# A two-layer hybrid trunk on one core: input groups projected in another order, key selection beside the gates, weight pieces ordered behind the splits of activations

## The chip, the cores and the metric

The kernel runs on one core of one Trainium2 chip. The metric is the device time of one launch in microseconds (us); smaller is better. The inputs lie in HBM as f32, the output goes back there as f32.

## What is computed

A trunk of two layers on one sequence of 256 tokens with 1024 channels. Each layer is `x += 1/2 FFN1(norm(x))`, `x += mixer(norm(x))`, `x += 1/2 FFN2(norm(x))`; a last RMSNorm follows. An FFN is `(silu(g) * u) @ w_down` with `g, u = split(h @ w_gu)` and 2816 hidden columns. The mixer is, cut to what matters:

```
(q_a,k_a,v_a,f_a, q_b,k_b,v_b, q_c,c_kv, q_i,k_i,w_i, gates) = split(h @ w_in)
y_a = forgetting_attention(6 heads)         # softmax with a forget bias
y_b = stick_breaking_attention(5 heads)
k_c, v_c = split(rmsnorm(c_kv) @ w_kv_up)
score = sum_h relu(q_i @ k_i) * w_i         # the indexer, 4 heads
sel   = top_k(score, 64)                    # key selection
y_c = dsa_attention(5 heads over the selected keys)
merged = sum over a, b, c of sigmoid(gate) * (y @ w_up)
return merged @ w_out
```

## The kernel before

**Tiling.** All weight matrices are streamed once, as f32 chunks `raw` (1024 KB or less) that SyncE's queue loads into four buffers. Each chunk is cut into pieces of up to 128x1024; `emit_piece` (L258) calls `split` (L249) for each, which makes two fp16 parts: ScalarE writes `whi` (L251), then VectorE writes the rest, `wlo` (L253). Fourteen pieces of each may stand ready (`HL_BUFS`); `advance` keeps that many ahead of TensorE in program order. A product takes three fp16 matmuls (weights' high part by the activation's high part `xThi` and low part `xTlo`, weights' low part by `xThi`), all in `project_T` (L339, weights stationary, 256 columns moving) or `project` (L374 to L376). Before the kernel's main stream ends, nearly all of TensorE's time goes there.

**Banks.** The products accumulate in four PSUM banks, two for a group of 512 output columns, so a group can start only when the group before the last one has been read out of its two banks. In an FFN the gate columns `g` are read by `gate(k)` (L655 to L662: `s` = `g` times the norm's row `R`, then Silu), the up columns `u` by L667. `gate` is tried ahead of each contraction step k of the `u` columns. In the first FFN, whose norm `R` comes late, it waits for step 6 if `R` isn't there yet.

**Mixer.** `IN_GROUPS` (L50) lists the column groups of `w_in` in the order in which they are projected: QI (indexer), VA (values and forget logits of the first heads), QC (sparse heads and latent), KA, QA, QB, QB2, VB. After each, tasks are made: generators that issue a bit of attention work at every step. `background()` (L307) steps them once or so for each weight piece, so that attention stands between the matmuls of the projections. The tasks are `indexer` (scores `is`, then eight rounds of top-k on VectorE, L915 and L916, then the mask `pen`), `forget`, `latent`, `fox_heads` (names ending in a), `stick_heads` (b), `dsa_heads` (c, which finishes the indexer and the latent first). In their names, `s` is a score matmul, `p` a softmax, `pp`/`pT` its transpose, `y` the value product, `c` the stick-breaking sums, `e` and `l` their logarithms. The indexer's rounds wait until the first heads have begun (`while "fox" not in X`). After the eight groups the six gate groups `gt0` to `gt5` follow, then the 12 sigmoids (L1162), the up-projections `up` of the three branches (evacuated at L1174, summed at L1177, split into `mT`), and `w_out` (matmuls `o`, which read `mT`).

**Norms.** `ss` (sum of squares by matmul), `gms`, a power on GpSimd, `rstd`, `dg` (a diagonal), `rb` (a matmul that spreads it into a row) and `R`.

**What sets the order.** A scheduler fixes at build time the order of the instructions of each engine, by dependences and by the order in which the code issues them; `behind` adds an ordering without data. At run time each engine takes its instructions in that order. The profile names the FFN tiles without layer (`gw_ffn_gu`, `s0w_ffn_gu`), the order views with one.

## Time and profile before

| | us |
|---|---|
| timed runs | 1142.18, 1143.40, 1143.76 |
| median | 1143.4 |
| profiled execution, its own time | 1145.33 |
| its span | 1143.5 |
| TensorE (PE) busy | 1113.5 (97%) |
| VectorE (DVE) busy | 799.3 (70%) |
| ScalarE (ACT) busy | 649.8 (57%) |

The profile is of one execution. An engine is busy while one of its instructions runs; the shares are means over stages that differ. A row of the view of waits gives, for an engine's line, what released it at last, the idle time in all, how many times, and the longest.

### The profile page before, as it was taken

Reading aid. Unit: us, or ns where it says so; the run is one execution under the profiler, and the core shown is the slowest. Engines: PE = TensorE matmul, PEld = TensorE weight load, DVE = VectorE, ACT = ScalarE, POOL = GpSimd, SP = SyncE. Lnnn points to the kernel's source line nnn. Section 1 sums busy time; section 2 is a strip of 40 time slices with the busy share of each in tenths; the row PEclk is TensorE's granted clock in tenths of the full one; section 3 lists DMA queues with packets and bytes.
Section 4 is the critical chain, followed back from the end, with each engine's and each line's share of the span. In section 5 each row is a group of like instructions: output and inputs, shape, how many; then the busy total and the mean of one; then the engine's idle time right before and its main releaser. Section 6 shows DMA issues by size and latency. Waiting matters only on the chain.

```text
span 1143.5 us, 23671 instructions
## 1 busy us (share of the span) xinstructions
PE 1113.5 (97%) x9746; PEld 960.4 (84%) x9746; DVE 799.3 (70%) x1757; ACT 649.8 (57%) x1040; POOL 12.5 (1%) x25
## 2 busy tenths in 40 slices
PE   9999999999999899999999999999999999999996
PEld 8888887778888788888888888868788888888765
DVE  6966656898677876575676575579976789666733
ACT  7845545677667464464454464466766766644520
POOL 1000000000000000000000000000000000000000
PEclk9999999999999899999999999999999999999998
DMA  9956655555343765577656476556533448556801
GB/s 316 368 174 217 227 172 174 161 182 176 111 139 112 244 223 164 181 231 235 199 186 183 151 238 200 178 168 190 180 130 111 148 148 295 176 165 197 256 1 41
DMA packets 118762, 210.02 MB, mean 184 GB/s; under 512 B 4802, under 2 KB 43892, under 8 KB 118644
## 3 DMA queue, kind: packets, MB, share of 16 engines
q1 hardware_dynamic: 118324, 207.88, 56.1%
q8 instruction: 78, 1.28, 0.5%
q10 hardware_dynamic: 320, 0.53, 0.1%
q14 instruction: 40, 0.33, 0.1%
HBM read 207.35 MB, written 1.05 MB: 182 GB/s over the span
## 4 chain that ended last, share of the span: by engine, by line
PE 77%; DVE 13%; ACT 6%; issue 2%; DMA 1%; POOL 0%; POOLq 0%; DVEq 0%; ACTq 0%
PE gw_ffn_gu L339 19%; PE uw_ffn_gu L339 19%; PE d512w_ffn_down L339 8%; PE d0w_ffn_down L339 8%; PE gt L339 6%; DVE wlo L253 5%; PE o L339 3%; ACT whi L251 2%; PE in L376 2%; PE in L374 1%; PE in L375 1%; DMA raw<-in_w_ffn_gu_dram 1%; ACT gt L1162 1%; PE in L339 1%; DVE gt L1174 1%
## 5 line engine op out<-in xcount | busy, mean ns | idle before, releaser
L253 DVE SCALAR_TENSOR_TENSOR wlo<-raw,whi 128x1024 f16<-128x1024 f32 (+6 forms) x425 | 476.2, 1128 | 258.7 <-ACT whi L251 255.5
L251 ACT ACTIVATE whi<-raw 128x1024 f16<-128x1024 f32 (+6 forms) x425 | 411.4, 978 | 378.9 <-PE uw_ffn_gu L339 93.4
L339 PEld LDWEIGHTS <-whi 128*128 128x128 f16 x5504 | 537.7, 98 | 72.1 <-issue 8.3
L339 PEld LDWEIGHTS <-wlo 128*128 128x128 f16 x2768 | 271.2, 98 | 34.2 <-issue 1.8
L339 PE MATMUL gw_ffn_gu<-xThif,whi 128*128 128x256 f16 x704 | 191.8, 273 | 2.0 <-DVE s0w_ffn_gu L660 1.4
L339 PE MATMUL gw_ffn_gu<-xThif,wlo 128*128 128x256 f16 x704 | 191.5, 273 | 0.6 <-DVE wlo L253 0.6
L339 PE MATMUL uw_ffn_gu<-xThif,wlo 128*128 128x256 f16 x704 | 191.9, 273 | 0.0
L339 PE MATMUL uw_ffn_gu<-xThif,whi 128*128 128x256 f16 x704 | 191.9, 273 | 0.0
L339 PE MATMUL uw_ffn_gu<-xTlof,whi 128*128 128x256 f16 x704 | 191.9, 273 | 0.0
L339 PE MATMUL gw_ffn_gu<-xTlof,whi 128*128 128x256 f16 x704 | 191.7, 273 | 0.0
L339 PE MATMUL gt<-xThimx,whi 128*128 128x256 f16 x384 | 104.8, 273 | 0.0
L339 PE MATMUL gt<-xThimx,wlo 128*128 128x256 f16 x384 | 104.7, 273 | 0.0
L339 PE MATMUL gt<-xTlomx,whi 128*128 128x256 f16 x384 | 104.7, 273 | 0.0
L339 PE MATMUL d0w_ffn_down<-ahw_ffn_gu,whi 128*128 128x256 f16 x264 | 72.0, 273 | 0.0
L339 PE MATMUL d0w_ffn_down<-alw_ffn_gu,whi 128*128 128x256 f16 x264 | 72.0, 273 | 0.0
L339 PE MATMUL d512w_ffn_down<-alw_ffn_gu,whi 128*128 128x256 f16 x264 | 72.0, 273 | 0.0
L339 PE MATMUL d512w_ffn_down<-ahw_ffn_gu,wlo 128*128 128x256 f16 x264 | 72.0, 273 | 0.0
L339 PE MATMUL d0w_ffn_down<-ahw_ffn_gu,wlo 128*128 128x256 f16 x264 | 72.0, 273 | 0.0
L339 PE MATMUL d512w_ffn_down<-ahw_ffn_gu,whi 128*128 128x256 f16 x264 | 72.0, 273 | 0.0
L339 PE MATMUL o<-mT,whi 128*128 128x256 f16 x256 | 45.1, 282 | 4.2 <-ACT mT L251 3.2
L339 PE MATMUL in<-xThimx,whi 128*128 128x256 f16 x176 | 48.0, 273 | 0.0
L339 PE MATMUL in<-xThimx,wlo 128*128 128x256 f16 x176 | 48.0, 273 | 0.0
(329 smaller groups left out, 1400.7 us busy)
## 6 DMA issues: line engine op xcount, KB each, us to landing
raw<-in_w_ffn_gu_dram SPq DMA_DIRECT2D x61, 1024.0 KB, 5.4
raw<-in_w_ffn_down_dram SPq DMA_DIRECT2D x39, 1024.0 KB, 5.1
raw<-in_w_in_dram SPq DMA_DIRECT2D x26, 1024.0 KB, 5.0
raw<-in_w_ffn_gu_dram SPq DMA_DIRECT2D x32, 768.0 KB, 4.6
raw<-in_w_in_dram SPq DMA_DIRECT2D x12, 768.0 KB, 4.5
raw<-in_w_out_dram SPq DMA_DIRECT2D x8, 1024.0 KB, 5.1
raw<-in_w_ffn_down_dram SPq DMA_DIRECT2D x7, 512.0 KB, 3.8
raw<-in_w_in_dram SPq DMA_DIRECT2D x4, 896.0 KB, 4.8
```

The costliest lines, as they stand in the source:

```text
L251: a = nc.scalar.activation(hv, src, AF.Copy, scale=scale)
L253: return a, nc.vector.scalar_tensor_tensor(lv, src, scale, plain(hv), op0=ALU.mult, op1=ALU.subtract, **more)
L339: m = nc.tensor.matmul(o, u, v[:, k, :], start=(k == 0 and q == 0 and b % 2 == 0), stop=(end and q == len(ops) - 1))
L374: nc.tensor.matmul(o, a, wh, start=(k == 0), stop=False)
L375: nc.tensor.matmul(o, a, wl, start=False, stop=False)
L376: state["last"] = nc.tensor.matmul(o, b, wh, start=False, stop=(k == lastk))
L1162: i = behind(nc.scalar.activation(v, v, AF.Sigmoid), *(exps if sig0 is None else [sig0]))
L1174: nc.vector.scalar_tensor_tensor(v, pair(ps[i], 2), 1.0 / (sw * sy), v, op0=ALU.mult, op1=ALU.mult)
```

## The change

Four parts. (1) The groups are projected in the order VA, KA, QA, QB, QB2, VB, QI, QC, and the tasks of the indexer, the latent and the sparse heads are made after their groups, that is after those of the first and the stick-breaking heads. (2) The indexer steps three times, not twice, ahead of each pair of score heads, the wait for the first heads is gone, and the second pair of the first heads starts five steps late rather than three. (3) `state["urgent"]`: the split of the next weight piece is ordered behind the last parts of a norm, and behind the split of `mT`, on either engine. (4) `gate` is forced from step 3 in the first FFN and from step 4 elsewhere, where it was step 6. The same work is issued as before.

```diff
-IN_GROUPS = [(QI, 324), (VA, 390), (QC, 448), (KA, 384), (QA, 384), (QB, 384), (QB + 384, 256), (VB, 320)]
+IN_GROUPS = [(VA, 390), (KA, 384), (QA, 384), (QB, 384), (QB + 384, 256), (VB, 320), (QI, 324), (QC, 448)]
...
         r = split(hv, lv, src, sw, guard and guard.weight())
+        for own, first in zip(r, state.pop("urgent", ())):
+            behind(own, first)
...
-                    self.parts(k, xT[:, k, :])
+                    state["urgent"] = self.parts(k, xT[:, k, :])
...
-                if s or (norm.R is None and k < 6):
+                if s or (norm.R is None and k < (3 if isinstance(norm, FirstNorm) else 4)):
...
-                yield
-                yield
+                for _ in range(3):
+                    yield
...
-            while "fox" not in X:
-                yield
...
-            X["fox"] = True
...
-        group(*IN_GROUPS[0], [(0, 324, False, PQI)])
-        t_idx = Task(indexer(), True)
-        group(*IN_GROUPS[1], [(0, WA + HA, False, PVA)])
+        group(*IN_GROUPS[0], [(0, WA + HA, False, PVA)])
         t_f = Task(forget(), True)
-        group(*IN_GROUPS[2], [(0, WC, True, PQC), (WC, P, False, PCKV)])
-        t_lat = Task(latent(), True)
         norm.need(True)
-        for g, at, eighth in ((3, 3, False), (4, 0, True)):
+        for g, at, eighth in ((1, 3, False), (2, 0, True)):
...
-            Task(later(fox_heads(hs, f"a{l}"), 3 * (i == 1)))
-        for hs in pairs(HC):
-            Task(dsa_heads(hs, f"c{l}"))
+            Task(later(fox_heads(hs, f"a{l}"), 5 * (i == 1)))
...
         for hs in pairs(HB):
             Task(stick_heads(hs, f"b{l}"))
+        group(*IN_GROUPS[6], [(0, 324, False, PQI)])
+        t_idx = Task(indexer(), True)
+        group(*IN_GROUPS[7], [(0, WC, True, PQC), (WC, P, False, PCKV)])
+        t_lat = Task(latent(), True)
+        for hs in pairs(HC):
+            Task(dsa_heads(hs, f"c{l}"))
...
-                            split(mh[:, k:k + 2, :], ml[:, k:k + 2, :], v0, sm, note())
+                            state["urgent"] = split(mh[:, k:k + 2, :], ml[:, k:k + 2, :], v0, sm, note())
```

Three places where the order of instructions differs follow; a row is line, operation, written tile <- read tiles, shape.

**First FFN, VectorE.** Here `s0` and `s1` are the two gate reads of the first chunk and `wlo15` to `wlo18` pieces of the stream. Before:

```order
L253 SCALAR_TENSOR_TENSOR wlo15_301,sums_71<-raw11_294,whi15_300 128x1024
L660 TENSOR_TENSOR s0w_ffn1_gu0_0_483<-gw_ffn1_gu0_0_0_172,Rf1_0_486 128x512
L253 SCALAR_TENSOR_TENSOR wlo16_307,sums_71<-raw12_304,whi16_306 128x1024
L253 SCALAR_TENSOR_TENSOR wlo17_311,sums_71<-raw12_304,whi17_310 128x1024
L660 TENSOR_TENSOR s1w_ffn1_gu0_0_490<-gw_ffn1_gu0_0_1_173,Rf1_0_486 128x512
L667 TENSOR_TENSOR s0w_ffn1_gu0_0_483<-uw_ffn1_gu0_0_0_388,s0w_ffn1_gu0_0_483 128x512
```

Changed:

```order
L253 SCALAR_TENSOR_TENSOR wlo15_301,sums_71<-raw11_294,whi15_300 128x1024
L253 SCALAR_TENSOR_TENSOR wlo16_307,sums_71<-raw12_304,whi16_306 128x1024
L253 SCALAR_TENSOR_TENSOR wlo17_311,sums_71<-raw12_304,whi17_310 128x1024
L662 TENSOR_TENSOR s0w_ffn1_gu0_0_436<-gw_ffn1_gu0_0_0_172,Rf1_0_439 128x512
L662 TENSOR_TENSOR s1w_ffn1_gu0_0_443<-gw_ffn1_gu0_0_1_173,Rf1_0_439 128x512
L253 SCALAR_TENSOR_TENSOR wlo18_349,sums_71<-raw13_314,whi18_348 128x1024
```

`s0` has moved from behind `wlo15` to behind `wlo17`, and `s1` stands right after it.

**Mixer of the first layer, VectorE, key selection.** `m8` are the maxima of a round, `isc` the scores. Before, two of the eight rounds:

```order
L915 MAX m80_0_1_3058<-isc0_2612 128x8
L915 MAX m80_128_1_3061<-isc0_2612 128x8
L253 SCALAR_TENSOR_TENSOR wlo107_3037,sums_71<-raw58_2837,whi107_3036 128x1024
L916 MATCH_REPLACE isc0_2612<-m80_0_1_3058,isc0_2612 128x128
L916 MATCH_REPLACE isc0_2612<-m80_128_1_3061,isc0_2612 128x256
L915 MAX m80_0_2_3088<-isc0_2612 128x8
L915 MAX m80_128_2_3091<-isc0_2612 128x8
L253 SCALAR_TENSOR_TENSOR wlo108_3065,sums_71<-raw59_2897,whi108_3064 128x1024
L916 MATCH_REPLACE isc0_2612<-m80_0_2_3088,isc0_2612 128x128
```

Changed, the last round and what follows it:

```order
L915 MAX m80_0_7_3747<-isc0_3531 128x8
L915 MAX m80_128_7_3750<-isc0_3531 128x8
L916 MATCH_REPLACE isc0_3531<-m80_0_7_3747,isc0_3531 128x128
L916 MATCH_REPLACE isc0_3531<-m80_128_7_3750,isc0_3531 128x256
L850 TENSOR_TENSOR kcT0_3758<-kcTp0_3755,kcT0_3758 64x256
L919 TENSOR_SCALAR pen0_3753<-isc0_3531 128x384
L821 TENSOR_TENSOR Tc00_3766<-qc00_3763,Tc00_3766 64x256
L812 TENSOR_TENSOR gt0_2371<-gt0_0_1_3442,Rmx_0_2462 128x512
L253 SCALAR_TENSOR_TENSOR wlo119_3777,sums_71<-raw64_3318,whi119_3776 128x1024
```

Before, the rounds stand between pieces and other attention work; in the changed program all eight stand in one row of 32, behind the last `isc` sum, ahead of the mask `pen`, of `Tc00` (operand of the sparse heads' first score `sc00`) and of the read of the gate bank `gt0_0_1`. No piece stands between `wlo118` ahead of this block and `wlo119` behind it.

**End of the gates, ScalarE.** `gt0` is sigmoid in place (the gate tile of layer 0), `eb` and `y0` are the last stick-breaking steps. Before:

```order
L786 ACTIVATE eb04_4440<-eb04_4440 128x384
L1162 ACT_TABLE_LOAD
L1162 ACTIVATE gt0_2371<-gt0_2371 128x512 x3
L251 ACTIVATE y0_2989<-yb04_4545 64x256
L1162 ACTIVATE gt0_2371<-gt0_2371 128x512 x9
L251 ACTIVATE whi139_4568<-raw74_4280 128x1024
```

Changed:

```order
L1160 ACT_TABLE_LOAD
L1160 ACTIVATE gt0_2371<-gt0_2371 128x512
L251 ACTIVATE whi130_4267<-raw70_4035 128x1024
L1160 ACTIVATE gt0_2371<-gt0_2371 128x512 x4
L251 ACTIVATE whi131_4309<-raw70_4035 128x512
L1019 COPY pTc04_4303<-ppc04_4299 128x384
L1160 ACTIVATE gt0_2371<-gt0_2371 128x512 x3
L251 ACTIVATE whi132_4343<-raw71_4110 128x1024
L251 ACTIVATE y0_2712<-yc04_4337 64x256
L251 ACTIVATE whi133_4373<-raw71_4110 128x512
L251 ACTIVATE whi134_4401<-raw72_4211 128x1024
L251 ACTIVATE whi135_4435<-raw72_4211 128x512
```

The 12 sigmoids stood in one row behind the last attention work, ahead of `whi139`; now ten stand between pieces from `whi130` on and two behind `whi139`. Further on, the second `mT` pair moved from behind `whi151` to between `whi150` and `whi151`.

## Rows read from the trace of the kernel before

**Rows 1.** The page's chain of work that ended last, by engine.

```profile
PE 77%; DVE 13%; ACT 6%; issue 2%; DMA 1%; POOL 0%; POOLq 0%; DVEq 0%; ACTq 0%
```

**Rows 2.** Waits of PE: reader <- releaser: us in total, times, longest.

```profile
PE sa L860 <- ACT pa L786: 4.5, 2, 2.2
PE o L339 <- ACT mT L251: 3.2, 2, 2.7
PE is L860 <- DVE Tiq L819: 2.2, 2, 1.1
...
PE sc L860 <- ACT pa L786: 1.7, 2, 0.9
...
PE sb L860 <- DVE eb L1101: 1.3, 2, 0.7
PE o L339 <- DVE mT L253: 1.0, 2, 0.6
PE yc L990 <- ACT pTc L1019: 0.7, 2, 0.3
PE ya L990 <- ACT pTa L1019: 0.7, 2, 0.4
```

**Rows 3.** Windows: stretch, length, busy PE, PEld, DVE, ACT, POOL, granted clock, DMA share, GB/s.

```profile
30.00:36.00 6.00, 3.98 (x36) 3.27 (x34) 6.00 (x11) 5.90 (x9) 0.00 (x0) 1.00 1.01 355
250.17:253.59 3.42, 3.42 (x17) 2.35 (x17) 3.42 (x17) 2.47 (x5) 0.00 (x0) 0.50 0.58 159
379.88:386.70 6.82, 5.80 (x27) 3.88 (x27) 6.18 (x13) 3.13 (x5) 0.00 (x0) 0.50 0.37 111
813.37:816.78 3.41, 3.41 (x15) 2.18 (x14) 3.41 (x13) 2.13 (x5) 0.00 (x0) 0.50 0.85 264
```

**Rows 4.** Timeline of PE, first FFN: start, us, ..., [idle before <- releaser].

```profile
32.61 0.27 PE L339 MATMUL gw_ffn_gu<-xThif,whi 128*128 128x256 f16 x1 [1.37 <-DVE s0w_ffn_gu L660]
...
35.50 0.27 PE L339 MATMUL gw_ffn_gu<-xThif,whi 128*128 128x256 f16 x1 [0.65 <-DVE s1w_ffn_gu L660]
```

**Rows 5.** Timeline of DVE, first FFN.

```profile
31.87 0.68 DVE L660 TENSOR_TENSOR s0w_ffn_gu<-gw_ffn_gu,Rf 128x512 f32<-128x512 f32 x1
32.48 1.21 DVE L253 SCALAR_TENSOR_TENSOR wlo<-raw,whi 128x1024 f16<-128x1024 f32 x1
...
34.76 0.69 DVE L660 TENSOR_TENSOR s1w_ffn_gu<-gw_ffn_gu,Rf 128x512 f32<-128x512 f32 x1
```

**Rows 6.** Timeline of ACT, from the sigmoids to `w_out`, layer 0.

```profile
351.57 4.78 ACT L1162 ACTIVATE gt<-gt 128x512 f32<-128x512 f32 x9
...
377.96 2.00 ACT L251 ACTIVATE whi<-raw 128x1024 f16<-128x1024 f32 x2 [7.37 <-DMA raw<-in_w_ffn_gu_dram]
379.87 1.13 ACT L251 ACTIVATE mT<-gt 128x512 f16<-128x512 f32 x2
```

**Rows 7.** Timeline of SP's queue ahead of `w_out`, layer 0.

```profile
358.59 16.90 SPq L238 DMA_DIRECT2D raw<-in_w_ffn_gu_dram  x4
```

**Rows 8.** Timeline of DVE at two norms: mixer's of layer 0, then FFN2's.

```profile
193.98 0.22 DVE L533 TENSOR_SCALAR gms<-ssmx 128x1 f32<-128x1 f32 x2
...
195.86 0.48 DVE L547 TENSOR_SCALAR dgmx<-ident,rstdmx 128x128 f32<-128x128 f32 x2
...
412.01 0.17 DVE L544 TENSOR_SCALAR rstdf<-rstdf 128x2 f32<-128x2 f32 x1 [0.80 <-POOL rstdf L473]
```

**Rows 9.** Timeline of DVE, one round of top-k, layer 0.

```profile
229.51 0.61 DVE L915 MAX8 m<-isc 128x8 f32<-128x128 f32 x2
...
232.09 0.09 DVE L916 MATCH_VALUE_LOAD isc<-m,isc 128x8 f32 x1
...
232.42 0.41 DVE L916 MATCH_REPLACE8 isc<-m,isc 128x256 f32<-128x256 f32 x1
```

**Rows 10.** Timeline of PE, two matmuls in succession.

```profile
371.80 0.27 PE L339 MATMUL up<-y,whi 128*128 128x256 f16 x1
371.91 0.27 PE L339 MATMUL up<-y,wlo 128*128 128x256 f16 x1
```

More of the change, by code (lines that the diff above doesn't have):

```diff
@@ L1129, in mixer @@
         for i, hs in enumerate(pairs(HA)):
-            Task(later(fox_heads(hs, f"a{l}"), 3 * (i == 1)))
-        for hs in pairs(HC):
-            Task(dsa_heads(hs, f"c{l}"))
-        ps = group_T(*IN_GROUPS[5])
+            Task(later(fox_heads(hs, f"a{l}"), 5 * (i == 1)))
+        ps = group_T(*IN_GROUPS[3])
         for t in range(NT):
@@ L1139, in mixer @@
         scaled(qk[HD:, 8, :], ps[1][HD:, :SEQ], norm.R[HD:, :], False)
-        ps = group_T(*IN_GROUPS[6])
+        ps = group_T(*IN_GROUPS[4])
         scaled(qk[:, 9:11, :], pair(ps[0], 2), norm.by_row(2), False)
-        group(*IN_GROUPS[7], [(0, WB, False, PVB)])
+        group(*IN_GROUPS[5], [(0, WB, False, PVB)])
         for hs in pairs(HB):
             Task(stick_heads(hs, f"b{l}"))
+        group(*IN_GROUPS[6], [(0, 324, False, PQI)])
[4 more added lines that the diff above has]
+            Task(dsa_heads(hs, f"c{l}"))
         for i in range(6):
```

## The prediction

> **What bounds the kernel now.** I read the chain of work that ended last first: TensorE (PE) carries 77% of it [rows 1], and PE is busy for 97% of the span. The matmuls follow each other at 0.11 us [rows 10] and no part of the change takes one away. So the time can move in two ways only: PE's idle time, and the clock it is granted. The waits of PE come next. Apart from the start and the tail they sum to some 17 us, and the reader is to see that they lie in three places: two gate reads of the first FFN [rows 4], the attention work of both mixers, and the start of the second half of `w_out`, where `o` waits for `mT` [rows 2]. Then the windows: the granted clock is 1.00 (2.4 GHz) nearly everywhere, and 0.50 (1.2 GHz) in three stretches, each right behind a long stop. Two of 3.4 us follow the stops of 2.2 us at `sa`, one of 6.8 us follows the stop of 2.7 us at `o` in layer 0 [rows 2, 3]. A stretch at half clock costs half its length: 1.7 us and 3.4 us. After the 1.37 us stop of the first FFN the clock stays at 1.00 [rows 3, 4]. VectorE (DVE) is the engine most often waited for behind these stops: it never pauses in 30 to 36 us and in 250 to 254 us [rows 3].
>
> I make the sum as changes to the median of 1143.4 us. The profiled execution, 1145.33 us by itself and 1143.5 in its span, is 0.2% above that median; a term of a few us does not feel this.
>
> **First FFN: +5.6 us.** Forcing the gate at step 3 issues `s0` in the code sooner, but on DVE it now stands behind `wlo16` and `wlo17` rather than ahead of them. `wlo16` can't move forward, since `whi16` on ScalarE comes behind the copy of `R` in both programs. So `s0` takes the time slot of `s1`: it starts at about 34.7 us instead of 31.87, and `s1` follows 0.6 us later [rows 5]. The next gate chunk on PE needs the bank that `s0` reads. It began at 32.61 and did its first part until 34.85, where it stopped for `s1` (35.50 less 0.65) [rows 4]. Now it begins at 35.5, so 34.85 - 32.61 = 2.2 us of PE work move behind the stop, which grows from 1.4 to some 4.2 us; the stop for `s1` nearly goes, as its 0.6 us lie beside the first six matmuls. That is longer than any stop in the rows, so I charge the clock of the longest one, 2.7 us with 3.4 us of cost; the low end is 1.7. Together +5.6, at least +2.2 if the clock stays. The other FFNs' first reads show no wait in the trace, and gating them at step 4 is worth nothing; what hides them is that their norms are ready while the group before is projected.
>
> **`w_out`: -6.3 us.** Before, nine of the sigmoids run in one 4.8 us block on ScalarE, from 351.57 on, with `whi139` behind them [rows 6]; DVE has no piece to work on, later it has too much, raw buffers come free late, SP's next load goes out only at 358.59 [rows 7], and ScalarE waits 7.4 us for a load at 377.96 with the last `mT` behind that piece [rows 6]. In the changed order attention ends earlier, ten sigmoids lie between pieces, and the last `mT` stands ahead of `whi151`. I expect the 2.7 + 0.4 us of layer 0 and its 3.4 us of clock to go, and the 1.1 us of layer 1. What is late next is `wlo148`, which DVE takes ahead of the low part of `mT`; layer 1 already shows the stop of this kind, 0.6 us, so I leave 0.65 in each layer. Layer 0: -6.5 + 0.65; layer 1: -1.1 + 0.65; in sum -6.3. Bounds: -7.6 if that also goes, -2 if the loads stay late. Here too `urgent` acts. Its other use, the parts of a norm, gets nothing: PE shows no wait there.
>
> **Mixers, what goes.** The stops of before stand at places that no longer exist in that form. Per layer: `sa` 2.25 with 1.7 of clock, `is` 1.1, `sc` 0.87, `sb` 0.67, `ya` 0.35, `yc` 0.34 [rows 2, 3]: -7.3.
>
> **Mixers, what comes.** (a) Norm row. Before, the whole VA group stood between `ss` and `rb`; now 11 matmuls do, 11 x 0.11 = 1.2 us. From `gms` to the end of `dg` took 193.98 to 196.34 = 2.36 us; so PE waits 1.2 us. At FFN2's norm GpSimd's step left DVE idle for only 0.80 us, and the same steps would take some 0.65 less [rows 8]: 0.5. The neighbours of neither row are those of the changed order; I take 0.9. (b) Key selection. `dsa_heads` finishes the indexer at once, and nothing delays it any longer until the sparse heads are far off. All eight rounds then run in one block. One round is 0.54 us for the two maxima and 0.66 for the two replacements (from start to next start) [rows 9], so 1.2, and eight take 9.6. The relu, the last sum, `kcT`, `pen` and `Tc00` around them are six short steps of 0.3 to 0.4 us, as one MAX8: some 2.3. From `is3` to `sc00` that makes 11.9 us. PE has, between these two in its order, 84 gate matmuls (9.2 us) and `cb04` (some 0.5 by its columns): 9.7. A stop of 2.2 us, just that of `sa`, so its clock too: 3.9; the low end is 0 where DVE comes to the block with `is2` already summed, the high end 5 with another stretch of clock. Pieces don't run out meanwhile: by the order some nine of the fourteen are still ahead of PE. (c) Others. In the changed order attention cuts into the projection at about 25 places, in few matmuls each. At 14 of them, by counting the matmuls that lie between two dependent attention steps, the chain through ScalarE and DVE is longer than PE's work. Before there were five such places besides `sa`, and they stopped PE for 3.3 us, 0.67 each. 14 x 0.67 = 9.4 is the high end; 1.7, five places at the smallest of 0.34, the low one. A stop at one place lets the other engines get ahead for the next, so the 14 can't all count in full; I take half, 4.7.
>
> Per layer 0.9 + 3.9 + 4.7 - 7.3 = +2.2; both layers +4.4.
>
> **Sum.** 5.6 - 6.3 + 4.4 = +3.7: 1147.1 us, forecast 1147.
>
> The Trainium skill, "TensorE: Matmul & The Clock Gate", section "Why this matters for your kernels", lets the clock fall only after stops longer than those of 2.2 and 2.7 us here. By that rule the removed clock at `o` would be worth nothing, the two at `sa` and `sc00` would cancel as they do now, and the sum would be 3.4 us higher, 1150.5. The trace disagrees, 0.50 behind each of the three stops, and the measurement decides.
>
> **Rivals.**
> *Faster, about 1137.* The places of (c) are hidden as before, and the stop at `sc00` falls short of a lower clock: 0.5 + 2.2 + 1.7 - 7.3 = -2.9 per layer, so 5.6 - 6.3 - 5.8 = -6.5. For it: attention now starts earlier and has longer to spread, and before only five such places stopped PE. Against it: DVE is full in 250 to 254 us and its work is the same. It decides if the mixers' sum of new stops is below 7.3 per layer. The Trainium skill, "Perfetto Trace Analysis", section "Optimization Strategy", says that stages bound by different engines gain when they are interleaved. That speaks for this rival, since key selection now lies beside the gates; the order shows a solid block within them, which speaks against it.
> *No change, about 1143.* The mixers come out even, and the first FFN's loss meets `w_out`'s gain: 5.6 - 6.3 = -0.7.
> *Much slower, about 1160.* All places of (c) count, 9.4, and one of them falls together with another to a stop that lowers the clock, 1.7: 0.9 + 3.9 + 9.4 + 1.7 - 7.3 = +8.6 per layer, +17.2 - 0.7. It decides if DVE, rather than PE, sets the pace from QB to the gates.
> *The change doesn't do what it says* in one part already: the gate that is forced earlier is read later.
>
> **How the numbers follow.** A measurement of this kernel can tell about 0.2%, 2.3 us, from no change. Forecast 0.45, from 1141 to 1153 by the ends of its terms; faster rival 0.25; no change 0.15; much slower 0.15. The range takes in the forecast's and nearly all of the two outer rivals': 1137 to 1158, with one in ten left out on either side. Faster by over 0.2%: most of the faster rival with a little of the two middle cases, 0.28. Within 0.2%: most of "no change" and the forecast's lower part, 0.17. Slower: 0.55.
>
> **What would show it.** In the first FFN: PE's wait for `s0` of about 4.2 us and a clock of 0.50 behind it; if it is 2 us or less, that term is wrong. In `w_out`: `o` waiting for `mT` 0.7 us or less in both layers, no 7 us wait of ScalarE for a load, a clock of 1.00. In the mixers: `rb` waiting for `dg` by 0.5 to 1.2 us, `sc` waiting for `Tc` by about 2 us with the eight rounds in one block of 10 us on DVE, and many waits of 0.3 to 1 us at `pp`, `s`, `c` and `y`. If the sum of PE's waits in one mixer is below 5.6 us, the faster rival holds. What would make all of it wrong is a stop at a place where I counted PE's cover as enough, above all a piece that comes too late behind the block.

## The result, and the profile after

The changed kernel takes **1154.4 us** (median of three runs, 1152.80 to 1155.14) against 1143.4: a ratio of 1.0101, with an interval of 1.0085 to 1.0117. It is 11.0 us slower where 3.7 was forecast. Later medians of the kernel before lie at 1141.7 to 1142.2, against which the loss is 12.4 us. The time lies within the range and on the side that was held likelier; the size is three times the forecast, and it is nearer to the 1160 of the rival "much slower" than to 1147.

The page of the changed kernel, its busy times and its chain, answering [rows 1]:

```profile
PE 1125.5 (98%) x9746; PEld 963.9 (84%) x9746; DVE 801.5 (70%) x1757; ACT 649.8 (56%) x1040; POOL 10.2 (1%) x25
...
PE 84%; DVE 9%; ACT 5%; issue 1%; POOL 0%; POOLq 0%; DVEq 0%; ACTq 0%
```

PE's busy time grew from 1113.5 to 1125.5 us, by 12.0, as much as the loss, and no matmul was added. What PE doesn't spend busy went from 30.0 us of the span (1143.5 - 1113.5) to 27.1 (1152.6 - 1125.5). So PE stands idle for less time than before and is slower all the same. Against the second profile of the kernel before (experiment e9: busy 1110.9, not busy 29.2) the two changes are +14.6 and -2.1. That is what has to be explained.

The waits of PE after, answering [rows 2] (reader <- releaser: us in total, times, longest):

```profile
PE sc L862 <- DVE Tc L821: 4.3, 2, 2.1
PE gw_ffn_gu L341 <- DVE s0w_ffn_gu L662: 3.8, 1, 3.8
PE ppa L1017 <- ACT pa L788: 2.5, 4, 0.9
PE warm L428 <- POOL ident masks.py:199: 2.0, 1, 2.0
PE o L341 <- DVE mT L253: 1.3, 2, 0.6
PE rbmx L553 <- DVE dgmx L549: 1.2, 2, 0.6
```

The clock, answering [rows 3] (columns as there): full just ahead of the first FFN's stop, 0.50 (1.2 GHz) in three stretches ahead of the tail, one behind that stop and one behind each stop at `sc`.

```profile
34.00:35.18 1.18, 0.17 (x2) 0.16 (x2) 1.18 (x4) 0.77 (x1) 0.00 (x0) 1.00 1.09 378
35.18:38.59 3.41, 3.41 (x18) 2.45 (x17) 2.90 (x6) 3.38 (x5) 0.00 (x0) 0.50 1.02 381
304.83:308.25 3.42, 3.42 (x19) 2.47 (x18) 3.36 (x6) 0.52 (x1) 0.00 (x0) 0.50 0.23 27
868.03:871.44 3.41, 3.41 (x19) 2.45 (x17) 3.35 (x7) 0.52 (x1) 0.00 (x0) 0.50 0.21 58
```

Where the time went, by the lengths of the stages: from the first PE matmul of one to the first of the next. The first column, the gate and up columns of FFN1, is taken from the start of the span. A mixer's stage begins with the `w_down` of the FFN1 ahead of it, which takes 57.64 us before and after alike, and ends at the first `up`; the length of a mixer given below is that of this stage, unless a window is named. The row "before again" is a second profile of the kernel before (experiment e9); the changes are taken against it.

| us | FFN1 (gate, up) | `w_down`, mixer 0 | up, `w_out` 0 | FFN2, next FFN1 (gate, up) | `w_down`, mixer 1 | up, `w_out` 1 |
|---|---|---|---|---|---|---|
| before, the profile of the rows | 128.03 | 222.59 | 48.90 | 290.85 | 222.59 | 44.26 |
| before again | 128.21 | 222.56 | 44.25 | 290.84 | 223.64 | 44.25 |
| after | 131.28 | 228.66 | 43.59 | 290.69 | 228.67 | 43.59 |
| change | +3.07 | +6.10 | -0.66 | -0.15 | +5.03 | -0.66 |

In sum +12.7, about the 12.4 of the medians; what comes behind these stages is 0.2 us shorter. The mixers hold 11.1 of it.

Now one mixer in both profiles: windows from the norm's `ss` to the first `up`, layer 0, first of the kernel before and then of the changed one (columns as in [rows 3]).

```profile
192.36:350.62 158.26, 152.62 (x1288) 127.13 (x1287) 127.74 (x347) 108.87 (x239) 3.24 (x3) 0.99 0.50 157
```

```profile
196.86:359.94 163.08, 158.26 (x1287) 128.71 (x1287) 126.79 (x346) 113.22 (x248) 2.08 (x3) 0.99 0.48 154
```

Idle is the length less PE's busy time: 5.64 us before, 4.82 after. The clock's mean is the same, 0.99. Busy time grew by 5.64 us with as many matmuls, and with fewer columns: of two groups of columns, each projected ahead of `ss`, the changed kernel leaves out of its window VA (7.94 us), the kernel before QI (6.69), so on equal terms the stretch is 6.1 longer, not 4.8.

To see what "busy" hides I took the time from each PE start to the next, less the shortest tenth of that kind of matmul (the same for both kernels), and put what is left to a stop (the trace shows PE idle), to half clock, or, where neither applies, to the rest:

| mixer 0, us | stops | half clock | rest |
|---|---|---|---|
| before | 6.78 | 1.66 | 8.23 |
| after | 6.68 | 1.67 | 14.43 |

The whole loss of the mixer, 6.2 us, is in the rest. Where the line between stop and rest is drawn moves up to 1.8 us from one column to the other; the rest grows by some 6 us in any case. There it lies at the matmuls of attention and those around them: `yc` 1.47 to 2.71, `ya` 1.43 to 2.51, `yb` 1.37 to 1.92, `cb` 0.35 to 1.10, `pp` 0.01 to 1.02. What changed for them is their company. I call it a visit when matmuls of one kind of tile stand in a row on PE. A mixer had 85 such rows before, among them 9 visits of value products `y`; it has 122 after, 17 of them of `y`. The projection itself is interrupted hardly more often, 44 times against 41; what grew are the changes within these interruptions. Two visits on PE's timeline (start, duration); the kernel before has all twelve value matmuls of a pair of heads in one, between two gate matmuls:

```profile
281.09 0.27 PE L339 MATMUL gt<-xThimx,wlo 128*128 128x256 f16 x1
281.29 1.15 PE L990 MATMUL ya<-pTa,pr 128*64 128x128 f32 x12
282.37 0.28 PE L339 MATMUL gt<-xThimx,whi 128*128 128x256 f16 x1
```

In the changed kernel a pair is cut up, with transposes `pp` of another pair between:

```profile
247.55 0.30 PE L378 MATMUL in<-whi,xTlomx 128*128 128x324 f16 x1
247.82 0.33 PE L1017 MATMUL ppa<-ident,pa 128*128 128x128 f32 x1
248.08 0.43 PE L990 MATMUL ya<-pTa,pr 128*64 128x128 f32 x2
248.44 0.44 PE L1017 MATMUL ppa<-ident,pa 128*128 128x128 f32 x2
248.81 0.65 PE L990 MATMUL ya<-pTa,pr 128*64 128x128 f32 x4
249.39 0.31 PE L376 MATMUL in<-whi,xThimx 128*128 128x324 f16 x1
```

No idle time stands beside any of these rows, since the recorded end of a matmul is past the start of the next one (0.27 us long, 0.11 from start to start [rows 10]). The Trainium skill, "Perfetto Trace Analysis", section "Tensor Engine Instruction (MATMUL, LD_WEIGHTS)", says that the end on this engine is estimated from the instruction's size, not observed; the rows agree. A loss of 0.1 or 0.2 us at a change of kind disappears under such an end, and is called busy.

### The profile page after: what moved, and what is told of

Its sections match the earlier page's. It is cut to its first block, busy times and chain, and to the rows that moved or that the text cites. A ratio compares the mean times of both kernels' runs of the same rounds, so it can differ in the third digit from the quotient of the medians.

```text
span 1152.6 us, 23700 instructions
## 1 busy us (share of the span) xinstructions
PE 1125.5 (98%) x9746; PEld 963.9 (84%) x9746; DVE 801.5 (70%) x1757; ACT 649.8 (56%) x1040; POOL 10.2 (1%) x25
## 3 DMA queue, kind: packets, MB, share of 16 engines
q8 instruction: 78, 1.28, 0.5%
HBM read 207.35 MB, written 1.05 MB: 181 GB/s over the span
## 4 chain that ended last, share of the span: by engine, by line
PE 84%; DVE 9%; ACT 5%; issue 1%; POOL 0%; POOLq 0%; DVEq 0%; ACTq 0%
PE gw_ffn_gu L341 20%; PE uw_ffn_gu L341 20%; PE gt L341 8%; PE d0w_ffn_down L341 8%; PE d512w_ffn_down L341 7%; DVE wlo L253 3%; PE o L341 3%; PE in L341 2%; ACT whi L251 2%; PE up L341 1%; DVE gt L1172 1%; DVE isc L916 1%; PE in L378 1%; PE in L376 1%; PE in L377 1%
## 5 line engine op out<-in xcount | busy, mean ns | idle before, releaser
L341 PE MATMUL in<-xTlomx,whi 128*128 128x256 f16 x176 | 48.0, 273 | 0.0
```

What stands on the lines that cost most here:

```text
L341: m = nc.tensor.matmul(o, u, v[:, k, :], start=(k == 0 and q == 0 and b % 2 == 0), stop=(end and q == len(ops) - 1))
```

## The experiments

**The theory** after the result: the mixers lose by PE's changes from one kind of matmul to another, at a price for each visit, and not by stops or clock. **Its rivals**: the stop at `sc` with its half clock is what the mixers lose; or many short waits, each too small to be seen. For the other stages: the earlier gate costs the first FFN 3 us; and the gain in `w_out` comes from `urgent`, or from the order of attention's end.

**e1: the gate of the first FFN from step 6 again, all else as changed.**

```diff
-                if s or (norm.R is None and k < (3 if isinstance(norm, FirstNorm) else 4)):
+                if s or (norm.R is None and k < (6 if isinstance(norm, FirstNorm) else 4)):
```

> The changed kernel with the gate of the first FFN forced at step 6 again, all else as changed. Theory of the prediction with the size that the two traces show: PE's stop for s0 goes from 3.79 us back to 1.37 + 0.65 us and the stretch at half clock behind it (3.41 us, cost 1.7) goes; the first FFN ends 3.25 us sooner, 1154.4 - 3.3 = 1151.1. Rival, the term as it was predicted: -5.6, 1148.8. Rival, the gate is not the cause (the pieces are): no change, 1154.4.

1151.44 us, ratio to before 1.0084 (1.0064 to 1.0105): 3.0 less than the changed kernel, and the first FFN ends at 128.21 as in "before again". Part 4 costs what its stage shows. Against my reading of the clock stands a row of this run: in its layer 0 the stop at `sc` is as long as in the changed kernel,

```profile
301.35 0.39 PE L862 MATMUL sc<-kcT,Tc 128*128 128x256 f32 x1 [2.12 <-DVE Tc L821]
```

but no half clock follows (the stretch behind it):

```profile
301.67:305.08 3.41, 3.29 (x29) 2.67 (x28) 3.35 (x6) 0.88 (x3) 0.00 (x0) 1.00 0.19 17
```

That mixer is only 0.84 us shorter for it (227.82 against 228.66). So half clock is not what the mixers lose.

**e7: the kernel before with part 4 alone.** The same edit the other way round (`k < 6` to 3 and 4).

> The kernel before with the fourth part alone (the gate forced at step 3 in the first FFN, step 4 elsewhere). Theory: s0 stands behind wlo16 and wlo17, PE's stop grows from 1.37 + 0.65 to 3.8 us with 3.41 us at half clock behind it: +3.0 to +3.3, 1146.6, ratio 1.0028; the other FFNs show nothing. Rival, the stop comes from the other parts: ratio 1.000.

1144.26 us, ratio 1.0015 (1.0004 to 1.0026), +2.05. The stop for `s0` is 3.66 us, as long as in the changed kernel, but in this profile the half clock behind it lasts twice as long:

```profile
34.65:41.48 6.83, 6.01 (x29) 4.16 (x29) 6.14 (x13) 6.70 (x8) 0.00 (x0) 0.50 1.04 370
```

The profiled execution took 1146.30, 2 us above the median; half of 6.83 - 3.41 is 1.7. So the loss of the first FFN differs between executions: 4.8 us in this profile (132.99 against 128.21), 3.1 in that of the changed kernel, 3.0 by the medians of e1 and 2.05 by those here, below the 3.0 to 3.3 expected. How long the clock stays low makes 1.7 us of that; the rest of the spread stays open.

**e2: attention's matmuls kept in the order in which the code issues them, all else as changed.** Each is ordered behind the attention matmul before it, so that a pair's value products are not cut up.

```diff
+        def whole(m):
+            behind(m, *said[-1:])
+            said.append(m)
+            return m
...
-                    m = nc.tensor.matmul(o, v(h, ks), w[:, i * P:(i + 1) * P], start=(i == 0), stop=(i == 2))
+                    m = whole(nc.tensor.matmul(o, v(h, ks), w[:, i * P:(i + 1) * P], start=(i == 0), stop=(i == 2)))
...
-            for i in range(3):
-                nc.tensor.transpose(ps[:, i * P:(i + 1) * P], p[:, i * P:(i + 1) * P], ident)
+            for i in (1, 2, 0):
+                whole(nc.tensor.transpose(ps[:, i * P:(i + 1) * P], p[:, i * P:(i + 1) * P], ident))
```

> The changed kernel, with the attention matmuls of a mixer kept on PE in the order in which the code issues them, the transposes and the stick-breaking sums begun with the operand that comes last; same matmuls, same number. PE then changes from one kind of matmul to another 80 times in a mixer instead of 122 (the kernel before: 85). Theory of switches: the mixers lost 6.1 us each, not by stops (the idle time fell from 5.6 to 4.8 us per mixer) but by the 37 changes of kind more, some 0.17 us each, that the view of waits does not show; so 42 fewer give 6 to 7 us back per mixer, 1140 to 1143. Theory of stops, as predicted: the stops at sc (2.1 us and 1.7 for the clock) and the others stay, so 1152 to 1155; if the fixed order adds stops, slower.

1148.97 us, ratio 1.0064 (1.0043 to 1.0085). The rows of one kind fall from 122 to 80, and a mixer from 228.7 to 226.0 us. That is 2.7 less each, where 6 to 7 were to go if that were all. By the sorting above, the rest fell from 14.4 to 10.3 us and the stops rose from 6.7 to 8.3; idle in the window is 160.42 - 154.23 = 6.19 us.

```profile
196.73:357.15 160.42, 154.23 (x1287) 128.26 (x1287) 127.06 (x346) 113.41 (x248) 2.11 (x3) 0.99 0.49 157
```

```profile
PE yb L1000 <- ACT eb L798: 5.9, 6, 2.0
...
PE ppa L1027 <- ACT pa L798: 3.5, 4, 1.4
```

The theory gets its sign right, two thirds of its size in the rest and two fifths in time; a part of what a kept order saves returns as waiting, now for the exponential `eb`, which a looser order had worked around.

**e6: the kernel before, with the value products cut in two and nothing else.** The second head of a pair makes its matmuls a step later. Their operands have long been there, so no wait of data is added.

```diff
-            for h, w in zip(heads, ws):
+            def one(h, w):
...
+            one(heads[0], ws[0])
+            Task(rest(), True)
```

> The kernel before with one edit: the value products of a pair of heads are issued in two halves, the second head's three matmuls at the next step, with 3 to 24 projection matmuls between them; all other steps stay where they were. PE goes to the value products 16 times in a mixer instead of 9, with the same matmuls. Theory of switches: each visit costs 0.35 us more than its matmuls (0.09 ahead, 0.11 at the first, 0.15 behind it), so 7 x 0.35 = 2.5 us per mixer, +4.9 in all, 1148.3, ratio 1.004, and PE's idle time by the view of waits does not rise by as much. Rival, visits are free and only stops count: ratio 1.000.

1149.06 us, ratio 1.0055 (1.0034 to 1.0077). Visits of `y` go from 9 to 16 in a mixer, and each mixer takes 227.5 us instead of 222.6: +4.9. Of that, stops are +0.3, half clock is +0.7, and the rest rose from 8.2 to 12.1, by 3.9 us: 0.56 for each of seven visits, where 0.35 was expected. The profiled execution, 1150.40, is 1.3 us above the median; by the medians a mixer loses 3.4. One visit of half the size on its timeline:

```profile
283.35 0.27 PE L339 MATMUL gt<-xThimx,wlo 128*128 128x256 f16 x1
283.55 0.87 PE L991 MATMUL ya<-pTa,pr 128*64 128x128 f32 x6
284.35 0.28 PE L339 MATMUL gt<-xThimx,whi 128*128 128x256 f16 x1
```

From the gate matmul ahead to the one behind takes 1.00 us for six value matmuls, and took 1.28 for twelve. Two halves take 2.00, less 0.11 for the gate matmul that stands once more in it: 1.89 against 1.28, 0.61 us for the cut. Both ways of reading agree.

But the cut does two things: it adds a visit, and it parts the two heads of a pair. The kernel before has a visit of one head too, the odd one of the sparse heads, and it takes the same 1.00:

```profile
313.08 0.27 PE L339 MATMUL gt<-xThimx,wlo 128*128 128x256 f16 x1
313.29 0.87 PE L990 MATMUL yc<-pTc,kvc 128*64 128x128 f32 x6
314.09 0.28 PE L339 MATMUL gt<-xThimx,whi 128*128 128x256 f16 x1
```

Its six starts are 0.11 us apart, with 0.05 more at the first and 0.10 more at the last, and at its entry 0.20 us pass from the gate matmul to it instead of 0.11: 0.24 us for a visit. The twelve of a pair take only 1.08 where twice six would take 1.31 and the same 0.15 at the ends, because in the middle of their row the trace has starts some 0.05 us apart, which a row of one head nowhere has. So of the 0.61 us some 0.24 is the price of a visit, and some 0.37 is that the matmuls of two heads no longer run side by side.

In the changed kernel two of the seven pairs of a mixer still have their twelve in one row. Eight added visits at 0.24 and five parted pairs at 0.37 make 3.8 us; the starts of the `y` matmuls and of those ahead of them show 3.8 to 3.9 more than before (the `y` matmuls alone 12.23 against 9.36). That is some 60% of the 6.2 us. Short waits for data are not what is paid there: the 0.20 us at the entry is the same whether the profile names a releaser or none (last section). That `pp`, `cb` and the like pay for their visits is argued from their rows alone.

**e3: key selection spread, all else as changed.** The sparse heads step the indexer and the latent rather than finish them at once.

```diff
-            for t in (t_idx, t_lat):
-                t.finish()
+            while not (t_idx.done and t_lat.done):
+                for t in (t_idx, t_lat):
+                    t.done or t.step()
+                yield
```

> The changed kernel, but the sparse heads step the indexer and the latent on and come back later, instead of finishing them at once: the eight rounds of top-k stand between pieces, three at a time. Theory of stops: the stop at sc (2.13 us) and its stretch at half clock (1.7) go, -3.8 per mixer, 1146.8 as long as nothing else moves. With the theory of switches: the changes of kind fall from 122 to 106 as well, 16 x 0.17 = 2.7 per mixer more, 1141. Rival: the sparse heads now end in the last gate group, one to two groups later, the sigmoids again come in a block behind them, and the up-projections and w_out give back up to 6 us in layer 0 and 0.7 in layer 1: 1148 to 1153.

1146.98 us, ratio 1.0047 (1.0027 to 1.0067). The mixers are 3.8 us shorter each. The one stop of 2.1 us is gone and with it the half clock in both mixers, but the waiting is not: it is passed on to three smaller places (0.95 and 0.90 for `Tc`, 0.66 for `pc`), and idle in the window is 159.27 - 154.18 = 5.09 us, more than in the changed kernel.

```profile
196.59:355.86 159.27, 154.18 (x1288) 127.09 (x1288) 126.00 (x344) 113.28 (x248) 2.08 (x3) 1.00 0.49 159
```

```profile
PE sc L862 <- DVE Tc L821: 3.7, 4, 1.0
...
PE sc L862 <- ACT pc L788: 1.3, 2, 0.7
```

By the sorting, 1.7 of the gain is clock and 2.4 is the rest (14.4 to 12.0), with 106 rows of one kind instead of 122 and 12 visits of `y` instead of 17; the stops rose by 0.3. So this run, meant for the rival, can't tell the two apart by itself.

**e4: all of the change but `urgent`.** The two assignments of `state["urgent"]` are dropped.

> The changed kernel without its third part (no piece is ordered behind a norm's parts or the mT splits). Theory of the prediction: the parts of a norm get nothing from it; in w_out the mT split stands behind one or two more pieces on ScalarE, so o waits for mT by 0 to 2 us more per layer: 1154 to 1158. Rival: w_out's gain of 6.0 us comes from this part and not from the order of the groups: about 1160.

1154.92 us, ratio 1.0113 (1.0087 to 1.0140), no different from the changed kernel, with 43.59 us in `w_out` in both layers. No gain from part 3 can be measured, and the gain in `w_out` is not its doing.

**e5: the kernel before, with the sparse heads last to end.** Tasks of the sparse and the stick-breaking heads are made after the last group, in the order c, b, c, b, b, c.

```diff
+        for kind, i in [('c', 0), ('b', 0), ('c', 1), ('b', 1), ('b', 2), ('c', 2)]:
+            if kind == "b":
+                Task(stick_heads(pairs(HB)[i], f"b{l}"))
+            else:
+                Task(dsa_heads(pairs(HC)[i], f"c{l}"))
```

> The kernel before with one edit: the tasks of the heads are made after the last group in the order sparse 0, stick 0, sparse 1, stick 1, stick 2, sparse 2, so that a sparse head, not a stick-breaking one, is the last; groups, indexer, gates and pieces as before. In the first four runs up-projections and w_out took 43.59 us in both layers, with urgent or without it, and with attention ending in the fourth or in the last gate group; before 48.90 and 44.26. Theory of the last exponential: the sigmoids have to wait for the last exponential; a stick-breaking head has its last one right ahead of its value product, a sparse head two steps sooner, so the sigmoids start some 7 us earlier here as well: w_out -5.3 and -0.7, in all 1143.4 - 6 = 1137.4, ratio 0.995, if the mixers' stops stay. Rival, the early groups are needed for it: 48.9 and 44.3 stay, ratio 1.000. Other mixers' stops can move by 1 to 2 us per layer either way.

1141.83 us, ratio 0.9995 (0.9984 to 1.0006), and `w_out` at 44.21: the last exponential of the stick-breaking heads is not what holds it. What goes with the 0.66 us in all profiles here is where attention's last value product stands. It stands right ahead of the first `up` (its last matmul starts 0.2 us earlier) in the kernel before, e5, e6, e7, e10 and e11, and the stage takes 44.2 us or more; it stands 2.8 us or further ahead in the changed kernel, e1 to e4, e8 and e12, and the stage takes 43.59 or 43.60. No run moved this alone, so the cause is not shown; e12 has the groups of the kernel before, so their order is not needed for it.

**e9: the kernel before, profiled again.**

> The kernel before, unchanged, profiled a second time. In the first profile its up-projections and w_out took 48.90 us in layer 0 and 44.26 us in layer 1, with one load (the one that whi150 waits for) 7.5 us on its way in layer 0 and 5.3 us in layer 1; kernels e6 and e7, which leave this part as it was, took 44.25 in both, their load 5.1 us. Theory: the 4.6 us were an event of that one execution, so layer 0 takes 44.2 to 44.3 us here, o waits for mT by some 1.1 us and the clock stays at 1.00 there. Rival: they belong to the kernel before, and e6 and e7 escaped them by chance of their shift: 48 to 49 us again.

1142.02 us. In layer 0 `w_out` takes 44.25 us, as in layer 1, not the 48.90 of [rows 6]. ScalarE waits 5.23 us for the load where it waited 7.37, PE's waits are short, and the clock stays at 1.00:

```profile
375.83 2.00 ACT L251 ACTIVATE whi<-raw 128x1024 f16<-128x1024 f32 x2 [5.23 <-DMA raw<-in_w_ffn_gu_dram]
```

```profile
378.41 0.27 PE L339 MATMUL o<-mT,whi 128*128 128x256 f16 x1 [0.38 <-ACT mT L251]
...
379.42 0.27 PE L339 MATMUL o<-mT,whi 128*128 128x256 f16 x1 [0.75 <-DVE mT L253]
```

```profile
379.00:386.00 7.00, 6.58 (x61) 5.89 (x61) 7.00 (x15) 2.00 (x2) 0.00 (x0) 1.00 0.62 216
```

The 2.7 us stop at `o` and its 6.8 us of half clock belonged to that one execution, in which the load took 7.46 us instead of 5.17; e5, e6, e7 and e10, too, take 44.2 to 44.3 us in both layers.

**e8: e1, e2 and e3 together.**

> The changed kernel with three things mended together: gate at step 6 in the first FFN, attention matmuls kept in issue order, top-k spread between pieces. Alone they gave -3.0, -5.4 and -7.4 us. If they add: 1154.4 - 15.8 = 1138.6, ratio 0.996. The last two overlap in the changes of kind (122 to 80 and to 106; together 82) and each has stops of its own that it adds, so more likely 1141 to 1144, ratio 0.998 to 1.001. If it is above 1146, the groups' order itself costs something that neither stops nor changes of kind show.

1143.48 us, ratio 1.0009 (0.9998 to 1.0019): no difference from the kernel before can be measured. One by one the three give 3.0, 5.4 and 7.4, in sum 15.8; together 10.9. e2 and e3 save in part the same rows of one kind. With 82 of these and 9 visits of `y` the rest is 9.2 us, within 1 us of the kernel before, and no half clock is left in layer 0 (layer 1 has one stretch of 3.41 us); but the stops, 6.8 before, are 9.3 (all of layer 0). The mixers stay at 224.4 and 225.0 us.

**e10 to e12: can the kernel before gain from this?** In e10 the third pair of the first heads starts a step later, the heads of b and c alternate, and the two gate reads `s0` and `s1` follow each other.

> The kernel before with three edits of its own kind: the third pair of the first heads starts one step (24 projection matmuls, 2.6 us) later; sparse and stick-breaking heads alternate, so that all attention still ends within the gates; s0 and s1 of a gate are read one right behind the other. Theory: the stop at sa (2.2 us) and the half clock behind it (1.7) go in both mixers, -7.8, and the stop for s1 (0.65) goes, while PE's changes of kind stay at 88 against 85 (+0.5 per mixer): about -7.5, ratio 0.9935, 1134.5 beside 1142. Rival: other stops take the place of the one at sa (as in all kernels so far, where a mixer's idle time stayed at 4.8 to 7 us whatever the order): ratio 0.998 to 1.002.

1143.64 us, ratio 1.0012 (1.0003 to 1.0020), as the rival said. It was aimed at the wrong pair: the stop at `sa` belongs to the second, and it stayed. e11 delays the second pair by five steps, keeps the order of attention as in e2, and reads `s0` and `s1` in succession.

```diff
-            Task(later(fox_heads(hs, f"a{l}"), 3 * (i == 1)))
+            Task(later(fox_heads(hs, f"a{l}"), (0, 5, 0)[i]))
```

> The kernel before (its groups, its indexer) with the one part of the change that moves the second pair of the first heads five steps on instead of three, and with the attention matmuls kept in issue order and s0 and s1 read one behind the other. The run before this showed that the stop of 2.2 us is at the score of the second pair (sa02), not of the third, which it had moved for nothing. Theory: sa02 now stands 60 projection matmuls later, behind the first pair's value products, so its stop and the half clock behind it go, -3.9 per mixer, the changes of kind fall from 85 to 78 (-1 per mixer), s1's stop goes (-0.65): about -10, 1132, ratio 0.991. Rival, stops are only passed on: the third pair's and the sparse heads' steps now stand closer and stop PE by as much, ratio 0.998 to 1.002.

1139.59 us, ratio 0.9982 (0.9971 to 0.9993), again in the rival's range. The stop at `sa` is gone, and one of 2.56 stands at `ppa` in its place. e12 is e11 with the heads of b and c alternating (the loop of e5, in the order c, b, c, b, c, b).

> As e11_pair_five, with the sparse and the stick-breaking heads alternating. Theory: as e11 at sa02, and the steps of two kinds of heads give each other's chains time, 76 changes of kind: 1131 to 1134, ratio 0.990 to 0.993. Rival: the last product of both kinds falls into the last gate group together and the end of the mixer stops: ratio 0.996 to 1.000.

**1136.52 us**, ratio 0.9953 (0.9936 to 0.9970), 5.2 us below the kernel before and 17.9 below the changed one, between the range of its theory and that of its rival. The mixers take 221.5 us, `w_out` 43.6, and a mixer has 76 rows of one kind:

```profile
PE 1108.7 (98%) x9746; PEld 958.0 (84%) x9746; DVE 799.2 (70%) x1757; ACT 650.8 (57%) x1040; POOL 12.5 (1%) x25
```

```profile
PE ppa L1030 <- ACT pa L799: 7.5, 6, 2.6
PE is L873 <- DVE Tiq L832: 2.2, 2, 1.1
```

By the sorting, the rest of a mixer is 7.6 us and the stops are 6.1, both below the kernel before. Against "before again" the first FFN is 0.6 us shorter, the mixers 1.1 and 2.2, `w_out` 0.7 and 0.7; of the 2.2, 1.1 is that layer 1 was longer in that profile. Busy time is 2.2 us less than there (1110.9 - 1108.7) with the same 9746 matmuls. The largest stop left, 2.6 us at `ppa`, would be the next thing to move.

## Why the prediction was right in its direction and short in its size

**The step that failed** is the premise: "So the time can move in two ways only: PE's idle time, and the clock it is granted." It followed from the pace of 0.11 us in [rows 10], which holds inside a row of stream matmuls and not where attention enters or leaves. The prediction even counted the entries ("at about 25 places, in few matmuls each") and charged them only for stops. The term that was missing is 6.2 us per mixer: 3.8 for the value products, by their visits and their parted pairs (e6 and the rows beside it), and the remainder by rows alone. Against the forecast of +4.4 the two mixers gave +11.1: +12.4 from this term, the stops and the clock about even (6.68 + 1.67 against 6.78 + 1.66 us per mixer) where +4.4 was forecast for them, and -1.05 because layer 1 of "before again" was itself that much longer than [rows 2] show it. By stages the errors are -2.5 us in the first FFN, +5.0 in `w_out` and +6.7 in the mixers; 3.7 and these make 12.9, of which 12.7 were seen. The direction was right by luck: the terms that the prediction did have came to +3.1 in the first FFN, -1.3 in `w_out` and -0.2 for stops and clock in both mixers, +1.6 in all, less than the 2.3 us it could tell from no change. The time also lies above the 1153 to which the ends of the forecast's terms reached, and is within the range only because the range took in the rival "much slower".

Two readings of the rows were wrong as well. At most of the stops in [rows 2] it was ScalarE that released PE (`sa`, `o`, `sc`, `yc`, `ya`), not VectorE; no term rests on that. And that the profiled execution's 0.2% above the median does not touch a term of a few us did not hold: it had 4.65 us in `w_out` that the second profile doesn't have.

**First FFN, forecast +5.6, measured +3.1.** The mechanism is as described. On DVE `s0` has the place of `s1`, two pieces stand ahead of it, and PE stops 3.79 us, where 4.2 was worked out (compare [rows 4, 5]):

```profile
31.97 1.23 DVE L253 SCALAR_TENSOR_TENSOR wlo<-raw,whi 128x1024 f16<-128x1024 f32 x1
...
33.12 1.22 DVE L253 SCALAR_TENSOR_TENSOR wlo<-raw,whi 128x1024 f16<-128x1024 f32 x1
...
34.27 0.69 DVE L662 TENSOR_TENSOR s0w_ffn_gu<-gw_ffn_gu,Rf 128x512 f32<-128x512 f32 x1
34.87 0.68 DVE L662 TENSOR_TENSOR s1w_ffn_gu<-gw_ffn_gu,Rf 128x512 f32<-128x512 f32 x1
```

```profile
35.01 0.27 PE L341 MATMUL gw_ffn_gu<-xThif,whi 128*128 128x256 f16 x1 [3.79 <-DVE s0w_ffn_gu L662]
```

The size that was off is the clock behind it: 3.41 us at half clock, worth 1.7, where I took 6.8 and 3.4. The longer stretch exists too (e7's profile).

**`w_out`, forecast -6.3, measured -1.3 for both layers.** The 0.65 us of `o` waiting for DVE's `mT` came as said (0.63), but there was little to lose: the term rested on rows of one execution, and e9 shows the stage at 44.25 us without them. The twin in layer 1 of the same profile showed 1.1 us of waits at the same place and no half clock, and I read that as the smaller case rather than the usual one.

**Mixers, what goes, -7.3.** Right: none of those stops is left but `is`, 0.25 a layer.

**What comes.** (a) `rb` 0.63 where 0.9 was taken. (b) Key selection as described: eight rounds in one block, forecast 9.6 us, measured 293.59 to 303.06 = 9.47, the stop behind it 2.13 where 2.2 was forecast, with 3.4 us of half clock.

```profile
293.59 0.61 DVE L915 MAX8 m<-isc 128x8 f32<-128x128 f32 x2
...
302.65 0.41 DVE L916 MATCH_REPLACE8 isc<-m,isc 128x256 f32<-128x256 f32 x1
...
303.93 0.42 DVE L821 TENSOR_TENSOR Tc<-qc,Tc 64x256 fp32r<-64x256 f32 x1
```

(c) The other stops sum to 2.0 us, at the low end of 1.7 to 9.4, and not 4.7: the term that was sized worst in the mixers. So by PE's recorded waits what came is less than what went, as the faster rival wanted ("below 7.3 per layer"): 0.63 + 2.13 + 1.7 + 2.0 = 6.5. The prediction's own test, "If the sum of PE's waits in one mixer is below 5.6 us, the faster rival holds", was met with 4.8, and the time went the other way: the test looked at the wrong quantity.

**The rivals.** The faster one was backed by a rule of the Trainium skill ("Perfetto Trace Analysis", section "Optimization Strategy"), that interleaving stages bound by different engines may help. PE's idle time did fall here, by 0.8 us in a mixer; this case adds that finer interleaving has a price of its own on PE. The "much slower" one came nearer in its number than the forecast, but not by its mechanism: (c) gave 2.0 us and not 9.4, and DVE is busy for 126.8 of the 163.1 us of a mixer's window. "No change" failed with `w_out`. That one part doesn't do what it says is true of part 3, from which e4 shows no gain, and of the gate, whose earlier call is read later.

## What to carry to other kernels

Where an engine is 97% busy, count how often it changes between kinds of work, not only how long it waits: the same matmuls in more and smaller visits, with pairs that ran side by side parted, cost some 6 us in each mixer here, without a row of idle time, and it is seen only from start to start. An experiment that cuts a row in two is to be compared with a row that was that short already, so that the price of the visit and that of the parting are told apart. A stall that is taken away at one place is mostly passed to the next (e2, e3, e11 each traded one wait for others), so a reordering pays by what it does to visits and to the longest stop. A large term that rests on one row of one profile is to be checked against its twin, in the other layer or in a second profile, before it enters a sum.

## What the runs showed of the hardware that was not expected

- Cutting a pair's twelve f32 value matmuls into two visits of six costs 0.56 to 0.61 us (e6); a visit by itself costs some 0.24 (one head's row in the kernel before). At its entry the first weight load starts together with its own matmul; within a row a load starts 0.11 us ahead of it, with the matmul before. Two rows of the kernel before, a pair's and one head's; the 0.21 us are the same, and behind one of them the profile shows no wait (`issue`):

```profile
281.29 0.41 PEld L990 LDWEIGHTS ya<-pTa,pr 128*64 128x64 f32 x5 [0.21 <-ACT pTa L1019]
...
313.28 0.63 PEld L990 LDWEIGHTS yc<-pTc,kvc 128*64 128x64 f32 x6 [0.21 <-issue]
```

- Half clock followed stops of 2.13 and 3.79 us in the changed kernel, and did not follow one of 2.12 in e1; it followed stops of 2.57 at `ppa` in e12, and not the one of 2.57 there in layer 1 of e11. Behind stops of 3.79 and 3.66 us it lasted 3.41 us once and 6.83 once (e7).
- The same stop differs between executions of one kernel: `ya` in layer 1 waited 0.3 us in the profile of [rows 2] and 1.99 in the next, where the half clock of 3.41 us came behind `ya` rather than behind `sa`:

```profile
817.13:820.54 3.41, 3.41 (x15) 2.18 (x14) 3.41 (x16) 2.83 (x6) 0.00 (x0) 0.50 0.44 161
```

- The same 1024 KB load took 7.46 us in one execution and 5.17 in another, at the same place of the program, and with the stop and the clock that followed it cost 4.6 us.
